# Two halves of a token operand in one matmul, and two weight rests on GpSimd, in a two-layer decoder trunk

## The chip, the cores and the metric

The kernel runs on one core of a Trainium2 chip. Its engines work in parallel, each through its own queue in order: TensorE (PE; its weight loads are listed as PEld), VectorE (DVE), ScalarE (ACT), GpSimd (POOL) and the DMA queues, which are fed from SyncE (SP), ScalarE and GpSimd. The metric is the device time of one execution in microseconds (us), taken as the median over runs.

## The reference

A residual stream of 512 tokens by 1024 channels goes through two layers. The first has a gated short convolution, the second sliding-window attention with sinks over a shared K/V; each is followed by a SwiGLU block with 2816 hidden columns. All is float32.

```python
def swiglu(h, w_gate_up, w_down):
    g, u = jnp.split(h @ w_gate_up, 2, axis=-1)
    return (jax.nn.silu(g) * u) @ w_down

for l in range(DEPTH):                     # DEPTH = 2
    if l < N_A:
        mix = short_conv_mixer(rmsnorm(h, a_pre_norm[l]), a_w_in[l], a_conv_w[l], a_w_out[l])
        h = h + rmsnorm(mix, a_post_norm[l])
    else:
        ...                                # K/V, queries, attention with sinks, b_w_o
        h = h + rmsnorm(attn, b_post_norm[j])
    ff = swiglu(rmsnorm(h, ffn_pre_norm[l]), ffn_w_gate_up[l], ffn_w_down[l])
    h = h + rmsnorm(ff, ffn_post_norm[l])
```

The change lies in the first line of `swiglu`, the product with `w_gate_up`, in both layers.

## The kernel before

**Two parts for each float.** TensorE multiplies in the rounded type fp32r. To keep float32 accuracy, each operand is split into a rounded part, made by a ScalarE copy into fp32r (`whi`, `xhi`), and the rest, made by subtracting that part from the original (`wlo`, `xlo`). `mm3` (lines 190 to 193) makes a product from three matmuls into the same PSUM bank: rounded weight by token rest (L191), rounded weight by rounded token (L192), and weight rest by rounded token (L193). Rest by rest is left out.

**Gate pairs.** The first two of the 22 tiles of hidden columns are multiplied plainly (`pgu`). The other twenty go in ten pairs per layer, twenty pairs in all. A pair is a 2 x 2 block product: the rows of blocks are gate and up, the inner index is split into two halves of 512 channels, and the tokens into two halves of 256. It is done with seven block products instead of eight, in the order 1, 2, 6, 5, 7, 3, 4 (`gate_jobs`, line 973). Each of the seven uses one 128 x 1024 weight tile (a block, or a sum of blocks) and one factor of 512 channels by 256 tokens (a half, or a sum of halves), for the two tiles e = 0, 1 of the pair and four steps k over channels: 8 calls of `mm3`, 24 matmuls of 256 columns.

Products 1, 6, 7 and 4 add up in the chain X (two PSUM banks `gx`, one for each e, 256 of 512 columns used), 5 and 3 in the chain Z (`gz`), 2 in Y (`gy`); Y and Z had two half-used banks each too. After each product and each e, `take` (lines 995 to 1014) evicts what is due into `st` and `gr`: ScalarE copies X after 1 and 6 (L1001) and Z after 5 (L1005); VectorE adds after 2 (L1003), 7 (L1007) and 3 (L1009); after 4 VectorE multiplies the up half, negated, with the gate half in `gr` (L1012, twice for each e). Between 3 and 4, `gate` applies the SiLU on ScalarE (L1036, one instruction for each e). The next product of a chain can't start in a bank before the evictions that read it are done.

The token factors are made once for each layer in `factors` (line 364): for products 1, 2 and 3 they are parts of the split tokens themselves, for 6, 5, 7 and 4 sums of token quarters, split into a rounded half (L382) and a rest half (L383) that lie beside each other in one tile of 1024 columns (`halves`).

**The line of jobs.** A layer's seven-product jobs stand in one line (`in_line`, line 471). The pairs go 0, 1, 2, then the eleven jobs of down round 0, then 3, 4, down round 1 (seven jobs), 5, 6, down round 2, 7, 8, 9, down round 3. When job j has issued its matmuls and evictions, job j + 3 is prepared (`LINE_LEAD = 3`): ScalarE rounds its weights (L466), VectorE makes the rest (L467), and the next raw tile is fetched on SP into the oldest of seven raw buffers, once that is free. So in a pair the weights of the next pair's products 1, 2 and 6 are prepared behind its products 7, 3 and 4. Four tiles each of `whi` and `wlo` go round. Behind the preparation, `issue` puts one or more DMAs on the GpSimd queue; they sum weight blocks in DRAM (`hsum`) and are paced by the rounding just made. What is left of them goes out unpaced at the pair's end (`sum_on`). In pairs 1 to 5 and 7 of each layer two of the sums are not made in DRAM but by VectorE on raw tiles (`Job.add`, L454), for products 6 and 3.

The activations of a finished pair become operands of the down rounds: `pair_sums` returns six late parts (a rounding L577 with its rest L578, sums L581 and L582, three splits L587 and L588), and one of them is issued behind each of the next jobs that are not marked `alone`. In pairs 8 and 9 `pair_acts` splits at once, behind product 4 (L1049 on ScalarE, L1050 on VectorE). Down jobs add their products into `mix` on VectorE (L636).

Each engine executes in the order written (`manual_schedule`), so a stage that waits holds up everything behind it on its engine.

Of the kernel before, what the change touches and what calls it, by code (L numbers as in the profile page):

```python
# [10 lines left out]
F32 = mybir.dt.float32  # L11
F32R = mybir.dt.float32r
AF = mybir.ActivationFunctionType
# [5 lines left out]
S = 512  # L19
# [53 lines left out]
def yoco_kernel(  # L73
# [165 lines left out]
    class Update:  # L239
# [124 lines left out]
        def factors(self):  # L364


            x = self.x[0]
            made = {p: [] for p in range(1, 8)}
            for p, k0, c in ((1, 0, 0), (2, 4, 0), (3, 4, 256)):
                made[p] = [[a[:, c : c + 256] for a in x[k0 + k]] for k in range(4)]  # L370
            for j in range(2):
                q11, q21, q12, q22 = (self.parts[i, hf, j] for hf in range(2) for i in range(2))

                nc.vector.tensor_tensor(out=q11, in0=q11, in1=q12, op=ALU.subtract)
                nc.vector.tensor_tensor(out=q12, in0=q22, in1=q12, op=ALU.subtract)
# [12 lines left out]
    class Ahead:  # L388
# [51 lines left out]
    class Job:  # L440
# [15 lines left out]
        def prepare(self):  # L456
            if not self.raws:
                return
            n = self.raws[0].n
            raw = self.raws[0].tile[:, :n]  # L460
            if self.slots:
                self.w = split_weights(None, raw, True)
                return
            hi = wsp.tile([P, D], F32R, tag="whi", name=name("whi"))
            lo = wsp.tile([P, D], F32R, tag="wlo", name=name("wlo"))
            self.begun = nc.scalar.activation(hi[:, :n], raw, AF.Copy)  # L466
            nc.vector.tensor_tensor(out=lo[:, :n], in0=raw, in1=hi[:, :n].bitcast(F32),  # L467
                                    op=ALU.subtract)
            self.w = hi, lo

# [481 lines left out]
    def ffn(l, before, ahead, gain, gpres, following):  # L952
# [20 lines left out]
        def gate_jobs(q, factors, out, to, then):  # L973

            sums = sums_of[f"g{l}{q}"]
            a21, a22, a11, a12 = (Raw(b) for b in sums.blocks)
            s1, s3, *rest = (Raw(b) for b in sums.sums)
            raws = {1: [a11], 2: [a12], 5: [s1], 7: [s3], 4: [a22]}  # L980
            if rest:
                raws[6], raws[3] = ([r] for r in rest)
            else:
                raws[6], raws[3] = [a11, s1], [a12, a11]
            chain = {1: "X", 6: "X", 7: "X", 4: "X", 5: "Z", 3: "Z", 2: "Y"}
            pools = {"X": ps_mm, "Y": ps_pt, "Z": ps_sc}
# [8 lines left out]
            def take(p, e):  # L995
                x, y, z = (banks[c][e][:, :256] if c in banks else None for c in "XYZ")
                gr = kept[2]
                g0, g1 = (gr[:, c : c + 256] for c in (e * S, e * S + 256))
                s, u = kept[e][:, :256], kept[e][:, 256:]
                if p in (1, 6):  # L1000
                    nc.scalar.activation(s, x, AF.Copy)  # L1001
                elif p == 2:
                    nc.vector.tensor_tensor(out=g0, in0=y, in1=s, op=ALU.add)  # L1003
                elif p == 5:
                    nc.scalar.activation(u, z, AF.Copy)  # L1005
                elif p == 7:
                    nc.vector.tensor_tensor(out=u, in0=x, in1=u, op=ALU.add)  # L1007
                elif p == 3:
                    nc.vector.tensor_tensor(out=g1, in0=z, in1=s, op=ALU.add)  # L1009
                else:  # L1010
                    for g, m in ((g0, x), (g1, u)):
                        nc.vector.scalar_tensor_tensor(out=g, in0=m, scalar=-1.0, in1=g,  # L1012
                                                       op0=ALU.mult, op1=ALU.mult)

            def run(p):
                def products(job):
                    if not kept:
                        kept.extend([slot("st"), slot("st"), wide("gr")])
                    whi, wlo = split[p] if p in split else job.w
                    c = chain[p]  # L1020
                    opened = c not in banks
                    if opened:
                        banks[c] = [bank("g" + c.lower(), pools[c]) for _ in range(2)]
                    for e in range(2):
                        for k in range(4):
                            kk = slice(e * S + k * P, e * S + (k + 1) * P)
                            mm3(banks[c][e][:, :256], whi[:, kk], wlo[:, kk], *factors[p][k],
                                opened and k == 0, k == 3 and p in (2, 3, 4),
                                skip_group_check=True)
                        take(p, e)  # L1030
                return products

            def gate():
                for e in range(2):
                    both = kept[2][:, e * S : (e + 1) * S]
                    nc.scalar.activation(both, both, AF.Silu)  # L1036
# [6 lines left out]
            return [Job(raws[p], run(p), {3: gate, 4: end}.get(p), len(raws[p]) > 1)  # L1043
                    for p in (1, 2, 6, 5, 7, 3, 4)]

        def pair_acts(gr, to):
            for c in (0, S):
# [543 lines left out]
```

## Time and profile before

| | |
|---|---|
| median of 3 runs | 1027.31 us (1027.06 to 1027.46) |
| the profiled execution | 1027.09 us, its span 1025.3 us |
| TensorE busy | 1016.4 us (99%), 6648 matmuls |
| VectorE busy | 823.7 us (80%), 1400 instructions |
| ScalarE busy | 577.4 us (56%), 1035 instructions |
| GpSimd busy | 195.8 us (19%), 259 instructions |
| granted TensorE clock | 0.998 of full speed |

The span runs from the first to the last instruction that the profile shows; the device time is some 2 us longer. A row of the timeline gives the start in us from the span's beginning, the duration in us, engine, line, operation, output and inputs by the program's names, shape, and how many instructions the row stands for; in brackets the idle time before it and what ended it. A row of a group gives the form, the count, the busy time in us, the mean duration in ns, and the idle time of the engine just before with what ended it. A row of a wait gives who waited, for whom, us in total, times, and the longest. A row of a window gives the stretch, its length, and for PE, PEld, DVE, ACT and POOL in turn the busy time in us and the instruction count, then the granted clock, the DMA share and GB/s. Ends of matmuls are modelled and overlap the next start, so the spacing of starts tells their cost.

### The profile page before, as it was taken

The page shows a single profiled execution, that of the slowest core. Times are in us where ns is not written, and L with a number is a line of the kernel's source. Part 1 is how long each engine was busy: PE and PEld are TensorE (multiplying, and loading weights), DVE is VectorE, ACT ScalarE, POOL GpSimd, SP SyncE. Part 2 cuts the span into 40 slices and gives each one's busy share as a digit, 9 for nine tenths or more (in the row PEclk, how much of TensorE's full clock was granted, in tenths as well). Part 3 has the DMA queues.
Part 4 walks back from the last instruction along what each step waited for, and adds up shares of the span by engine and source line. Part 5 has one row for each costly group of instructions (what it writes and reads, how often), then busy time and mean ns, then how long its engine had stood idle before and what let it go on. Part 6 is the DMA issues. An engine that isn't in the chain of part 4 may idle for free.

```text
span 1025.3 us, 17466 instructions
## 1 busy us (share of the span) xinstructions
PE 1016.4 (99%) x6648; PEld 925.8 (90%) x6648; DVE 823.7 (80%) x1400; ACT 577.4 (56%) x1035; POOL 195.8 (19%) x259
## 2 busy tenths in 40 slices
PE   9999999999999999999999999999999999999997
PEld 8888888999899898998897888889998999989986
DVE  5766767888688879878869998778886788887786
ACT  7323445865655454566476776677665554645642
POOL 0433033111111111000123653231111010110001
PEclk9999999999999999999999999999999999999999
DMA  9897699459978699779404789976889576988732
GB/s 353 293 268 224 181 255 350 135 169 291 338 246 291 200 313 319 254 220 307 164 9 156 186 246 268 233 280 153 275 282 326 167 263 208 311 286 259 243 135 83
DMA packets 66580, 244.59 MB, mean 239 GB/s; under 512 B 7872, under 2 KB 8384, under 8 KB 54720
## 3 DMA queue, kind: packets, MB, share of 16 engines
q1 hardware_dynamic: 51328, 145.98, 39.0%
q0 software_dynamic: 14592, 96.48, 36.7%
q8 instruction: 52, 0.85, 0.3%
q10 hardware_dynamic: 576, 1.02, 0.3%
q14 instruction: 32, 0.26, 0.1%
HBM read 237.15 MB, written 102.76 MB: 332 GB/s over the span
## 4 chain that ended last, share of the span: by engine, by line
PE 94%; DVE 4%; ACT 1%; DMA 1%; issue 0%; DVEq 0%; SPq 0%
PE gx L193 7%; PE gx L192 7%; PE gx L191 7%; PE gz L192 4%; PE gz L193 4%; PE gz L191 4%; PE pcub L191 4%; PE pcub L193 4%; PE pcub L192 4%; PE px L191 4%; PE px L192 4%; PE px L193 4%; PE pmix L193 3%; PE pmix L191 3%; PE pmix L192 3%; PE gy L191 2%
## 5 line engine op out<-in xcount | busy, mean ns | idle before, releaser
L467 DVE TENSOR_TENSOR wlo<-raw,whi 128x1024 fp32r<-128x1024 f32 x225 | 275.3, 1227 | 93.3 <-ACT whi L466 93.1
L466 ACT ACTIVATE whi<-raw 128x1024 fp32r<-128x1024 f32 x225 | 234.2, 1049 | 118.2 <-DVE raw L454 20.4
L192 PE MATMUL gx<-xt,whi 128*128 128x256 f32 x480 | 135.9, 283 | 0.0
L193 PE MATMUL gx<-xt,wlo 128*128 128x256 f32 x480 | 135.9, 283 | 0.0
L191 PE MATMUL gx<-xt,whi 128*128 128x256 f32 x480 | 135.9, 283 | 0.0
L192 PEld LDWEIGHTS gx<-xt,whi 128*128 128x128 f32 x480 | 92.2, 192 | 0.0
L193 PEld LDWEIGHTS gx<-xt,wlo 128*128 128x128 f32 x480 | 92.2, 192 | 0.0
L191 PEld LDWEIGHTS gx<-xt,whi 128*128 128x128 f32 x480 | 92.2, 192 | 0.0
L535 POOL DMA_DIRECT2D hsum<-in_w_gb_dram x96 | 63.5, 741 | 142.0 <-ACT whi L466 82.3
L1001 ACT ACTIVATE st<-gx 128x256 f32<-128x256 f32 x80 | 30.3, 383 | 82.6 <-PE gx L193 82.6
L535 POOL DMA_DIRECT2D hsum<-hsum x32 | 25.2, 789 | 264.3 <-ACT whi L466 209.1
L192 PE MATMUL pcub<-xhi,whi 128*128 128x512 f32 x168 | 65.4, 389 | 0.0
L191 PE MATMUL pcub<-xlo,whi 128*128 128x512 f32 x168 | 65.4, 389 | 0.0
L193 PE MATMUL pcub<-xhi,wlo 128*128 128x512 f32 x168 | 65.4, 389 | 0.0
L191 PE MATMUL px<-wlo,ahi 128*128 128x512 f32 x120 | 46.7, 390 | 0.0
L192 PE MATMUL px<-whi,ahi 128*128 128x512 f32 x120 | 46.7, 389 | 0.0
L193 PE MATMUL px<-whi,alo 128*128 128x512 f32 x120 | 46.7, 389 | 0.0
L192 PE MATMUL gz<-xt,whi 128*128 128x256 f32 x160 | 45.3, 283 | 0.0
L192 PE MATMUL gx<-xhi,whi 128*128 128x256 f32 x160 | 45.3, 283 | 0.0
L191 PE MATMUL gy<-xlo,whi 128*128 128x256 f32 x160 | 45.3, 283 | 0.0
L192 PE MATMUL gy<-xhi,whi 128*128 128x256 f32 x160 | 45.3, 283 | 0.0
L193 PE MATMUL gz<-xt,wlo 128*128 128x256 f32 x160 | 45.3, 283 | 0.0
(268 smaller groups left out, 3119.7 us busy)
## 6 DMA issues: line engine op xcount, KB each, us to landing
hsum<-in_w_gb_dram POOLq DMA_DIRECT2D x96, 512.0 KB, 8.0
raw<-hsum SPq DMA_DIRECT2D x88, 512.0 KB, 7.9
raw<-in_w_gb_dram SPq DMA_DIRECT2D x60, 512.0 KB, 7.5
hsum<-in_w_dn_dram POOLq DMA_DIRECT2D x36, 512.0 KB, 8.7
raw<-in_w_dn_dram SPq DMA_DIRECT2D x32, 512.0 KB, 6.7
hsum<-hsum POOLq DMA_DIRECT2D x28, 512.0 KB, 5.4
raw<-in_w_in_dram SPq DMA_DIRECT2D x21, 512.0 KB, 8.1
hsum<-in_w_dn_dram POOLq DMA_DIRECT2D x12, 768.0 KB, 12.7
```

The source lines that it names most:

```text
L191: nc.tensor.matmul(out, whi, xlo, start=start, stop=False, **kw)
L192: nc.tensor.matmul(out, whi, xhi, start=False, stop=False, **kw)
L193: nc.tensor.matmul(out, wlo, xhi, start=False, stop=stop, **kw)
L466: self.begun = nc.scalar.activation(hi[:, :n], raw, AF.Copy)
L467: nc.vector.tensor_tensor(out=lo[:, :n], in0=raw, in1=hi[:, :n].bitcast(F32), op=ALU.subtract)
L535: nc.gpsimd.dma_start(dst, src, max_dma_last_dim=4 * 4 * S, **kw))
L1001: nc.scalar.activation(s, x, AF.Copy)
```

## The change

In products 6, 7 and 4 the rounded token half and the rest half of a factor, which lie in one tile, are given to TensorE as one moving operand of two runs of 256 columns: one matmul with the rounded weights writes 512 columns of an X bank, the product with the rounded tokens into the first half and the product with the token rests into the second. A matmul of 256 columns with the weight rest follows. Product 1 still fills the first half only. The two halves are added when they are evicted: after 1 and 6 ScalarE copies the first half, and after 6 VectorE adds the second; after 7 VectorE adds both halves to `u` (four adds in place of two); after 4 ScalarE copies the first half, VectorE adds the second, and the multiplications follow. Chains Y and Z use one bank each for both e, their evictions are one instruction of 512 columns instead of two of 256, and so are the multiplications; the SiLU is one instruction of 1024. Evictions come once for each product, behind both e. In each pair the weight rests of the second and third job (products 2 and 6) are made by GpSimd instead of VectorE.

```diff
@@ Update.factors
                 for p, q in ((6, q22), (5, q11), (7, q12), (4, q21)):
-                    hi, lo = halves("xt", F32R)
+                    two = wide("xt", F32R)
+                    hi, lo = two[:, :S], two[:, S:]
+                    two = two.rearrange("p (i c) -> p i c", i=2)
                     nc.scalar.activation(hi, q, AF.Copy)
...
-                    made[p] += [[a[:, c : c + 256] for a in (hi, lo)] for c in (0, 256)]
+                    made[p] += [[hi[:, c : c + 256], lo[:, c : c + 256], two[:, :, c : c + 256]]
+                                for c in (0, 256)]
@@ Job
+        rest = nc.vector
...
-            nc.vector.tensor_tensor(out=lo[:, :n], in0=raw, in1=hi[:, :n].bitcast(F32),
+            self.rest.tensor_tensor(out=lo[:, :n], in0=raw, in1=hi[:, :n].bitcast(F32),
                                     op=ALU.subtract)
@@ gate_jobs
+            def take(p):
+                x, y, z = (banks.get(c) for c in "XYZ")
+                st, u, gr = kept
...
+                if p == 2:
+                    add(g0, tiles(y), tiles(st))
+                elif p == 5:
+                    nc.scalar.activation(u, z, AF.Copy)
+                elif p == 3:
+                    add(g1, tiles(z), tiles(st))
+                else:
+                    for e in range(2):
+                        a, b = x[e][:, :256], x[e][:, 256:]
+                        ste, ue = (v[:, e * 256 : (e + 1) * 256] for v in (st, u))
+                        if p == 7:
+                            add(ue, a, ue)
+                            add(ue, b, ue)
+                            continue
+                        nc.scalar.activation(ste, a, AF.Copy)
+                        if p != 1:
+                            add(ste, b, ste)
+                if p == 4:
+                    for g, m in ((g0, st), (g1, u)):
+                        nc.vector.scalar_tensor_tensor(out=g, in0=tiles(m), scalar=-1.0, in1=g,
                                                        op0=ALU.mult, op1=ALU.mult)
...
+                            if c == "X" and xboth:
+                                nc.tensor.matmul(banks[c][e], whi[:, kk], xboth[0], start=False,
+                                                 stop=False, **kw)
+                                nc.tensor.matmul(banks[c][e][:, :256], wlo[:, kk], xhi,
+                                                 start=False, stop=k == 3 and p == 4, **kw)
+                                continue
...
+                    take(p)
...
             def gate():
-                for e in range(2):
-                    both = kept[2][:, e * S : (e + 1) * S]
-                    nc.scalar.activation(both, both, AF.Silu)
+                nc.scalar.activation(kept[2], kept[2], AF.Silu)
...
+            for job in jobs[1:3]:
+                job.rest = nc.gpsimd
+            return jobs
```

More of the change, by code (lines that the diff above doesn't have):

```diff
@@ L993, in gate_jobs, with tiles, add @@
             banks, kept = {}, []
[L995 to L1003, printed above, removed]
+            def tiles(a):
+                return a.rearrange("p (e c) -> p e c", e=2)
+            def take(p):
+                x, y, z = (banks.get(c) for c in "XYZ")
+                st, u, gr = kept
+                g0, g1 = (gr.rearrange("p (e h c) -> p e h c", e=2, h=2)[:, :, h]
+                          for h in range(2))
+                def add(out, a, b):
+                    nc.vector.tensor_tensor(out=out, in0=a, in1=b, op=ALU.add)
+                if p == 2:
+                    add(g0, tiles(y), tiles(st))
                 elif p == 5:
                     nc.scalar.activation(u, z, AF.Copy)
-                elif p == 7:
-                    nc.vector.tensor_tensor(out=u, in0=x, in1=u, op=ALU.add)
                 elif p == 3:
-                    nc.vector.tensor_tensor(out=g1, in0=z, in1=s, op=ALU.add)
+                    add(g1, tiles(z), tiles(st))
                 else:
-                    for g, m in ((g0, x), (g1, u)):
-                        nc.vector.scalar_tensor_tensor(out=g, in0=m, scalar=-1.0, in1=g,
+                    for e in range(2):
[11 more added lines that the diff above has]
+                        nc.vector.scalar_tensor_tensor(out=g, in0=tiles(m), scalar=-1.0, in1=g,
                                                        op0=ALU.mult, op1=ALU.mult)
@@ L1022, in products @@
                     if opened:
-                        banks[c] = [bank("g" + c.lower(), pools[c]) for _ in range(2)]
+                        banks[c] = ([bank("gx", pools[c]) for _ in range(2)] if c == "X"
+                                    else bank("g" + c.lower(), pools[c]))
                     for e in range(2):
@@ L1026, in products @@
                             kk = slice(e * S + k * P, e * S + (k + 1) * P)
[L1027 to L1030, printed above, removed]
+                            xhi, xlo, *xboth = factors[p][k]
+                            kw = {"skip_group_check": True}
+                            if c == "X" and xboth:
[4 more added lines that the diff above has]
+                                continue
+                            out = (banks[c][e][:, :256] if c == "X"
+                                   else banks[c][:, e * 256 : (e + 1) * 256])
+                            mm3(out, whi[:, kk], wlo[:, kk], xhi, xlo,
+                                opened and k == 0 and (c == "X" or e == 0),
+                                e == 1 and k == 3 and p in (2, 3), **kw)
+                    take(p)
                 return products
             def gate():
-                for e in range(2):
-                    both = kept[2][:, e * S : (e + 1) * S]
-                    nc.scalar.activation(both, both, AF.Silu)
+                nc.scalar.activation(kept[2], kept[2], AF.Silu)
             def end():
@@ L1041, in end @@
                 return late
-            return [Job(raws[p], run(p), {3: gate, 4: end}.get(p), len(raws[p]) > 1)
+            jobs = [Job(raws[p], run(p), {3: gate, 4: end}.get(p), len(raws[p]) > 1)
                     for p in (1, 2, 6, 5, 7, 3, 4)]
+            for job in jobs[1:3]:
+                job.rest = nc.gpsimd
+            return jobs
         def pair_acts(gr, to):
```

## The prediction

> **What bounds the kernel now.** I read the page's busy times and chain first, then who waited for whom, then the start times of single instructions.
>
> ```profile
> span 1025.3 us, 17466 instructions
> ...
> PE 1016.4 (99%) x6648; PEld 925.8 (90%) x6648; DVE 823.7 (80%) x1400; ACT 577.4 (56%) x1035; POOL 195.8 (19%) x259
> ...
> PE 94%; DVE 4%; ACT 1%; DMA 1%; issue 0%; DVEq 0%; SPq 0%
> ```
>
> TensorE is busy for 99% and makes 94% of the chain. The waits of its weight loads say how little it stands still; the longest entry, and the only one on a weight rest:
>
> ```profile
> PEld psc L1273 <- issue: 4.7, 15, 0.7
> ...
> PEld px L191 <- DVE wlo L467: 0.3, 2, 0.2
> ```
>
> So a matmul taken away counts in full as long as nothing else becomes late. Busy times of matmuls overlap, so their price is read from starts (column 1):
>
> ```profile
> 408.89 0.39 PE L191 MATMUL px<-wlo,ahi 128*128 128x512 f32 x1
> ...
> 411.61 0.28 PE L191 MATMUL gx<-xlo,whi 128*128 128x256 f32 x1
> ...
> 417.36 0.28 PE L191 MATMUL gx<-xt,whi 128*128 128x256 f32 x1
> ...
> 420.24 0.28 PE L191 MATMUL gz<-xt,whi 128*128 128x256 f32 x1
> ```
>
> From 408.89 to 411.61 lie 12 products of 512 columns: 0.2267 us each. From 417.36 to 420.24 lie 24 of 256: 0.120. Two of 256 cost 0.240, 0.0133 more than one of 512.
>
> VectorE is next. In windows on gate pair 7 of layer 0 (its seven products) and on a down round:
>
> ```profile
> 411.60:431.76 20.16, 20.16 (x169) 20.14 (x168) 17.67 (x27) 12.91 (x20) 1.56 (x2) 1.00 0.81 258
> 333.16:352.23 19.07, 19.07 (x86) 15.78 (x85) 17.83 (x23) 6.37 (x6) 1.58 (x2) 1.00 0.83 262
> ```
>
> The fifth number is VectorE's busy time: 17.67 of 20.16 us. It has 2.5 us to spare in such a pair, 1.2 in a round.
>
> **The change, part by part.**
>
> ```profile
> L467 DVE TENSOR_TENSOR wlo<-raw,whi 128x1024 fp32r<-128x1024 f32 x223 | 273.9, 1232 | 93.3 <-ACT whi L466 93.1
> ...
> L192 PE MATMUL gx<-xt,whi 128*128 128x256 f32 x480 | 135.9, 283 | 0.0
> ...
> L636 DVE TENSOR_TENSOR mix<-mix,px 128x512 f32<-128x512 f32 x54 | 36.0, 685 | 5.6 <-PE px L193 5.2
> ...
> L1001 ACT ACTIVATE st<-gx 128x256 f32<-128x256 f32 x80 | 30.3, 383 | 82.6 <-PE gx L193 82.6
> ...
> L1036 ACT ACTIVATE gr<-gr 128x512 f32<-128x512 f32 x40 | 23.3, 625 | 25.7 <-DVE gr L1009 25.7
> ...
> L1003 DVE TENSOR_TENSOR gr<-gy,st 128x256 f32<-128x256 f32 x40 | 15.2, 417 | 0.0
> L582 DVE SCALAR_TENSOR_TENSOR s<-s,gr 128x256 f32<-128x256 f32 x36 | 15.2, 422 | 0.6
> ```
>
> *Products.* Products 6, 7 and 4 have 480 mm3 calls in 20 pairs (the row x480). Each loses one of its three matmuls, and 0.36 us becomes 0.2267 + 0.120: 480 x 0.0133 = **-6.4 us**. A 512-column product whose tokens come as two runs isn't in the trace; between 0.2267 (one run) and 0.240 (as two products) I take 0.2267, since it still is one instruction.
>
> *Evictions on VectorE.* Before, a pair has ten of 256 columns, two each in products 2, 7 and 3 and four in 4, at about 0.417: 4.2 us. After: 2 of 512 (0.685, L636's size), 8 adds of 256 (0.417) and 2 multiplies of 512 (0.7, some above L636) make 6.1. Against +1.9 stand two weight rests that leave, 2 x 1.23: about -0.5 us a pair, counted as nothing: it falls into the idle time above.
>
> *ScalarE.* Two more copies (2 x 0.383), one gate in place of two and one wide copy in place of two: some +0.4 us a pair beside 7 us idle. But the copies of product 4 are new ahead of the next weight rounding, which counts below.
>
> *The rests on GpSimd.* 38 of them (pair 0 has none for product 2). The page has no 128x1024 subtraction there; the same form with 512 columns, and what happens beside VectorE:
>
> ```profile
> 552.03 0.67 DVE L1213 TENSOR_TENSOR ra<-pq,ctab 128x512 f32<-128x512 f32 x1
> 552.22 1.29 POOL L1214 TENSOR_TENSOR sh<-sh,stab 128x512 f32<-128x512 f32 x1 [25.61 <-DVE sh L1211]
> ...
> 575.27 1.21 DVE L187 TENSOR_TENSOR wlo<-raw,whi 128x1024 fp32r<-128x1024 f32 x1
> ...
> 577.12 1.30 POOL L1221 TENSOR_TENSOR rlo<-ra,rhi 128x512 fp32r<-128x512 f32 x1 [2.01 <-ACT rhi L1220]
> ...
> 597.22 1.27 POOL L1214 TENSOR_TENSOR sh<-sh,stab 128x512 f32<-128x512 f32 x1 [3.93 <-DVE sh L1211]
> 597.62 1.95 DVE L187 TENSOR_TENSOR wlo<-raw,whi 128x1024 fp32r<-128x1024 f32 x1
> 598.57 2.16 POOL L1215 TENSOR_TENSOR ra<-ra,sh 128x512 f32<-128x512 f32 x1
> ```
>
> Bounds for one rest: 1.3 us and 2 x 1.30 = 2.6. I take 2.45, near the upper, for only a fixed start doesn't double. The last three rows matter most. VectorE's rest begins at 597.62 during a GpSimd product and takes 1.95 instead of 1.21: it ends 1.08 after GpSimd's end (598.49). GpSimd's next takes 2.16 instead of 1.30, for it stood behind that rest. The two exclude each other when both VectorE inputs lie in SBUF; with one in PSUM (552.03) VectorE runs at full speed.
> The Trainium skill, page "SBUF — State Buffer", section "SBUF: two separate sides", calls this port pair an exclusive lock held for a whole instruction, against VectorE operations with two SBUF inputs; these rows agree (1.95 against 1.21). By that rule the sum stays as below; without it, it would be 1027.1 - 6.4 = 1020.7.
> For the length, the Trainium skill, page "GPSIMD Engine Reference", section "Elementwise — side-by-side cycle accounting", gives 4497 ns for 2048 float32; half, 2.25, is an estimate by which the sum would be near 1027. No run here shows the size.
>
> *Where it hits.* In a pair the rests of the next pair's products 2 and 6 follow its products 3 and 4. Pair 7 to pair 8 before:
>
> ```profile
> 426.43 0.75 DVE L1007 TENSOR_TENSOR st<-gx,st 128x256 f32<-128x256 f32 x2
> 426.54 1.05 ACT L466 ACTIVATE whi<-raw 128x1024 fp32r<-128x1024 f32 x1
> 427.10 1.21 DVE L467 TENSOR_TENSOR wlo<-raw,whi 128x1024 fp32r<-128x1024 f32 x1
> ...
> 428.23 0.68 DVE L588 TENSOR_TENSOR alo<-s,ahi 128x512 fp32r<-128x512 f32 x1
> 428.83 0.75 DVE L1009 TENSOR_TENSOR gr<-gz,st 128x256 f32<-128x256 f32 x2
> 429.28 1.16 ACT L1036 ACTIVATE gr<-gr 128x512 f32<-128x512 f32 x2 [1.17 <-DVE gr L1009]
> ...
> 430.34 1.04 ACT L466 ACTIVATE whi<-raw 128x1024 fp32r<-128x1024 f32 x1
> ...
> 437.52 0.28 PE L191 MATMUL gx<-xt,whi 128*128 128x256 f32 x1
> ```
>
> After, by the same clock: the rounding of 426.54 ends at 427.7 (the wide copy ahead of it costs 0.1). GpSimd takes the port from 427.8 to 430.25, while VectorE finishes product 7's four adds (PSUM). Behind these stand product 1's rest, a split and product 3's add: the rest issues the next at 431.25, the add ends at 432.55, not 429.58. Then in line: gate to 433.6, product 4's copies to 434.2, the rounding for product 6 to 435.15, GpSimd's rest 435.25 to 437.7. Product 6 starts at 437.20 (437.52 less three savings of 0.107) and wants the rest at 437.43: **0.3 us lost**; 0.95 if the second multiply of product 4 gets the port first.
> Where the next pair also adds raw weights (1.22; pairs 1, 2, 4), VectorE goes on at 437.7: multiply 0.65, rest 1.14, split 0.35, add 0.6, rest 1.14, raw add 1.14, sums 0.85, and product 6's first add at 444.0; product 7 wants the bank at 443.15: **0.85 more**.
> From pair 8 to 9 the activations are split at once:
>
> ```profile
> 452.23 0.63 ACT L1049 ACTIVATE ahi<-gr 128x512 fp32r<-128x512 f32 x1 [0.69 <-DVE gr L1012]
> ...
> 453.58 0.36 ACT L1001 ACTIVATE st<-gx 128x256 f32<-128x256 f32 x1
> ```
>
> These two roundings wait for the blocked multiply (438.35 on that clock) and stand ahead of product 1's copies, which end 1.45 later, at 439.8; product 6 wants that bank at 437.2: **2.6 lost**.
> Per layer: 0 to 1, 1.15; 1 to 2, 0.85 (already late by then); 3 to 4, 0.6 (no split work behind pair 3); 5 to 6 and 7 to 8, 0.3 each; 8 to 9, 2.6: 5.8, and 11.6 for both.
>
> Where a down round precedes (3, 5, 7) I charge nothing:
>
> ```profile
> 352.59 1.28 DVE L636 TENSOR_TENSOR mix<-mix,px 128x512 f32<-128x512 f32 x2
> ...
> 356.67 1.23 DVE L467 TENSOR_TENSOR wlo<-raw,whi 128x1024 fp32r<-128x1024 f32 x1 [1.56 <-ACT whi L466]
> ```
>
> VectorE there works on PSUM and then idles 1.56 us for ScalarE; without this cover it would cost some 1 us each. Later raw fetches on SP (their buffers come free up to 4 us later) and the sums' issues on POOL (up to 2.5 us behind a rest) I cost at nothing: raws are fetched seven jobs ahead, some 20 us against 8 to land.
>
> **Sum.** The profiled execution took 1027.09 (span 1025.3 and 1.8 around it), 0.2 under the median. 1027.1 - 6.4 + 11.6 = **1032.3**.
>
> **Rivals.**
> *The waits stay in the slack* (faster). One quantity decides: the length of a GpSimd rest. Both rests lie on the path, so 0.1 us moves each boundary by up to 0.2. At 2.1 the waits come to some 4.4 and the gain leads by 2; at 1.3 hardly anything waits: 1021. For it: TensorE waited 0.3 in all for rests. Against: 1.30 at half the size. 1020.7 to 1025: 0.20.
> *Gain and waits cancel*, lengths of 2.1 to 2.3: 1025 to 1029: 0.15.
> *VectorE becomes the bound*: the port race goes against GpSimd at the ten boundaries with split work (+0.65 each), and the down rounds, with 1.2 us of slack, pay 1 each: 1027.1 - 6.4 + 11.6 + 6.5 + 6 = 1045. Against: 356.67's idle time. 0.09.
> *The wide product isn't cheaper* (0.240): the gain is gone, 1038.7. For it only that this operand shape isn't in the trace. 0.06.
>
> **Numbers.** My own case, 1029 to 1041, has 0.50. No change is what lies within 0.2% (2 us), about what a measurement of this kernel tells apart. Slower 0.50 + 0.09 + 0.06 = 0.65, same 0.15, faster 0.20. The range 1022 to 1046 leaves out the end of the first rival and a few cases above the third.
>
> **What the new profile would show.** Right: 480 fewer matmuls; starts 0.227 and 0.120 apart in turn; rests on POOL of some 2.45 us; VectorE rests stretched beyond 2 us beside them; weight loads or matmuls of gx waiting for POOL's rest, a VectorE add or a ScalarE copy, 10 us in all, the longest two at the last pair of each layer. Wrong: POOL rests near 2 us or less, VectorE's rests all at 1.23 us, no new TensorE wait, or weight waits on DMA.

## The result, and the profile after

| | before | after |
|---|---|---|
| median | 1027.25 us (1027.06 to 1027.46, 4 runs) | 1043.46 us (1040.87 to 1046.29, 4 runs) |
| the profiled execution, its span | 1027.09, 1025.3 us | 1042.82, 1041.0 us |
| ratio | 1 | 1.0157, interval 1.0144 to 1.0170 |
| granted clock over the span | 0.998 | 0.996 |

The changed kernel is 1.6% slower, 16.2 us by the medians, where 5 us had been forecast. Its runs also spread over 5.4 us, where those of the kernel before spread over 0.4.

The page of the kernel after: span, busy times, the chain by engine, and four groups.

```profile
span 1041.0 us, 16607 instructions
...
PE 1021.1 (98%) x6168; PEld 903.3 (87%) x6168; DVE 876.2 (84%) x1402; ACT 580.2 (56%) x1035; POOL 291.4 (28%) x297
...
PE 72%; DVE 16%; issue 4%; DMA 4%; ACT 3%; POOL 1%; DVEq 0%; ACTq 0%; POOLq 0%
...
L471 DVE TENSOR_TENSOR wlo<-raw,whi 128x1024 fp32r<-128x1024 f32 x187 | 253.3, 1360 | 51.6 <-ACT whi L470 51.5
L1049 PE MATMUL gx<-xt,whi 128*128 128x512 f32 x480 | 174.0, 401 | 5.7 <-ACT st L1025 4.5
L471 POOL TENSOR_TENSOR wlo<-raw,whi 128x1024 fp32r<-128x1024 f32 x38 | 95.8, 2522 | 226.1 <-ACT whi L470 170.0
...
L1030 DVE SCALAR_TENSOR_TENSOR gr<-st,gr 128x512 f32<-128x512 f32 x40 | 52.4, 1352 | 0.7
```

480 matmuls are gone, 6648 to 6168, and yet the span grew; TensorE's part of the chain fell from 94% to 72%, and VectorE's rose from 4% to 16%. VectorE lost 38 rests and is nevertheless busy for 876.2 us instead of 823.7: those that it kept take 1360 ns each instead of 1232.

TensorE's waits in the kernel after, where the kernel before had none on a gate product in this view (who waits, for whom, us in all, times, longest):

```profile
PE gx L1049 <- ACT st L1025: 4.5, 2, 2.3
PE gy L193 <- POOL wlo L471: 2.4, 2, 2.0
PE gx L1051 <- POOL wlo L471: 2.3, 3, 1.6
PE gx L1049 <- DVE st L1009: 1.2, 4, 0.3
```

These come to 10.4 us. The first row is the boundary from pair 8 to 9, once for each layer; the second and the 1.6 of the third are pair 7; what is left lies at the boundaries 0 to 1 and 1 to 2.

The timeline of the kernel after at the boundary 8 to 9 of layer 0:

```profile
457.02 1.06 ACT L1063 ACTIVATE gr<-gr 128x1024 f32<-128x1024 f32 x1 [4.28 <-DVE gr L1009]
...
457.99 0.64 ACT L1025 ACTIVATE st<-gx 128x256 f32<-128x256 f32 x2
...
458.51 1.06 ACT L470 ACTIVATE whi<-raw 128x1024 fp32r<-128x1024 f32 x1
...
459.65 2.48 POOL L471 TENSOR_TENSOR wlo<-raw,whi 128x1024 fp32r<-128x1024 f32 x1 [4.95 <-ACT whi L470]
...
459.78 2.89 DVE L1030 SCALAR_TENSOR_TENSOR gr<-st,gr 128x512 f32<-128x512 f32 x1
...
462.76 1.15 ACT L1079 ACTIVATE ahi<-gr 128x512 fp32r<-128x512 f32 x2 [3.19 <-DVE gr L1030]
...
463.82 0.64 ACT L1025 ACTIVATE st<-gx 128x256 f32<-128x256 f32 x2
...
464.24 0.50 PE L1049 MATMUL gx<-xt,whi 128*128 128x512 f32 x1 [2.25 <-ACT st L1025]
```

It is the chain of the prediction. GpSimd's rest starts 0.13 us ahead of the second multiply of product 4; that multiply takes 2.89 and ends 0.5 behind the rest; the two roundings of the activations, which need it, idle for 3.19; product 1's copies stand behind them, and TensorE stands still for 2.25 us for the bank.

The same kernel at pair 7 of layer 0, which the prediction charged with nothing:

```profile
412.83 1.06 ACT L470 ACTIVATE whi<-raw 128x1024 fp32r<-128x1024 f32 x1 [3.43 <-DMA raw<-in_w_gb_dram]
...
413.93 1.23 DVE L458 TENSOR_TENSOR raw<-raw,raw 128x1024 f32<-128x1024 f32 x1 [2.08 <-DMA raw<-hsum]
414.02 5.69 POOL L471 TENSOR_TENSOR wlo<-raw,whi 128x1024 fp32r<-128x1024 f32 x2 [10.44 <-ACT whi L470]
...
417.43 0.39 PE L193 MATMUL gy<-xhi,wlo 128*128 128x256 f32 x1 [2.02 <-POOL wlo L471]
...
417.85 2.94 DVE L471 TENSOR_TENSOR wlo<-raw,whi 128x1024 fp32r<-128x1024 f32 x1 [1.50 <-ACT whi L470]
```

The pair's first matmul starts at 412.13. The weights of its product 2 are rounded from 412.83 on, since their raw tile landed only then. VectorE's sum of raw tiles holds the port from 413.93, so GpSimd's rest, issued at 414.02, is finished at 417.4, and product 2, which wants it at 415.24, waits.

Windows of the kernel after (stretch, its length, busy time and count of PE, PEld, DVE, ACT and POOL, granted clock, DMA share, GB/s): the whole of pair 7 of layer 0 and the down round that answers to the one shown of before, and then three times two stretches of 3.41 us.

```profile
412.13:435.83 23.70, 21.68 (x145) 20.39 (x144) 18.57 (x23) 11.58 (x17) 9.60 (x5) 0.93 0.75 243
333.80:352.85 19.05, 19.05 (x86) 15.78 (x85) 18.80 (x26) 7.85 (x10) 4.48 (x3) 1.00 0.88 282
...
414.78:418.19 3.41, 1.39 (x12) 1.18 (x11) 1.91 (x4) 2.92 (x6) 3.41 (x2) 1.00 0.62 255
418.19:421.60 3.41, 3.41 (x18) 3.41 (x18) 2.94 (x2) 0.88 (x1) 3.04 (x3) 0.50 0.19 22
...
462.56:465.97 3.41, 1.73 (x9) 1.52 (x10) 1.93 (x4) 3.21 (x6) 0.00 (x0) 1.00 0.50 167
465.97:469.38 3.41, 3.41 (x27) 3.25 (x26) 3.41 (x6) 2.08 (x5) 0.00 (x0) 1.00 0.80 255
974.56:977.97 3.41, 1.50 (x9) 1.33 (x10) 1.93 (x4) 2.98 (x6) 0.00 (x0) 1.00 0.43 155
977.97:981.38 3.41, 3.41 (x15) 3.02 (x14) 3.16 (x5) 1.58 (x4) 0.00 (x0) 0.50 0.75 259
```

Pair 7 takes 23.70 us instead of 20.16; the down round takes as long as before (19.05, 19.07). Behind the wait of pair 7 the granted clock is 0.50 for 3.41 us: TensorE is busy all through, and its matmuls of 256 columns start 0.213 us apart instead of 0.120. The same happens behind the wait of pair 9 in layer 1 (977.97), and not behind that of layer 0 (465.97: clock 1.00), though that wait is no shorter.

The windows show what differs. In all profiles of this case the clock changes only at whole multiples of 3.413 us from its first change (the two drops here lie 559.78 us apart, 164 times as much). Of the wait in pair 7 2.02 us fall into one such stretch (3.41 less 1.39 busy), of that in pair 9 of layer 1 1.91, but of that in layer 0 only 1.68, for it lies across two stretches. In the profiles of the two kernels and of the experiments below there are ten such drops, and one at the end of each; every one follows a stretch with 1.82 us or more of idle TensorE, and no stretch with 1.78 or less is followed by one.

**Where the 15.7 us of span come from**, by the starts of the stages in the two profiles, layer 0 and layer 1 together:

| | us |
|---|---|
| 20 pairs, 20.00 us instead of 20.16 where nothing waits (2.9 of it in products 6, 7 and 4: 60 x 0.048) | -3.2 |
| boundaries 0 to 1 (0.99, 1.30) and 1 to 2 (0.53, 0.50) | +3.3 |
| boundary 3 to 4 | 0 |
| boundaries 5 to 6 and 7 to 8, 0.23 each | +0.9 |
| boundary 8 to 9 (2.5 each, 2.41 of it ahead of product 6) | +5.0 |
| pair 7 behind the down round (3.71, 2.44), 1.6 of it the low clock in layer 0 | +6.15 |
| low clock behind 8 to 9 of layer 1 | +1.5 |
| the two layer ends | +2.1 |
| start of the first pair, and the down rounds between | -0.2 |
| sum | 15.6 |

### The profile page after: what moved, and what is told of

It is laid out like the page before. It is cut to its first block, busy times and chain, and to the rows that moved or that the text cites. A ratio compares the mean times of both kernels' runs of the same rounds, so it can differ in the third digit from the quotient of the medians.

```text
span 1041.0 us, 16607 instructions
## 1 busy us (share of the span) xinstructions
PE 1021.1 (98%) x6168; PEld 903.3 (87%) x6168; DVE 876.2 (84%) x1402; ACT 580.2 (56%) x1035; POOL 291.4 (28%) x297
## 4 chain that ended last, share of the span: by engine, by line
PE 72%; DVE 16%; issue 4%; DMA 4%; ACT 3%; POOL 1%; DVEq 0%; ACTq 0%; POOLq 0%
PE gx L1049 7%; DVE wlo L471 4%; PE gx L1051 4%; DMA raw<-in_w_gb_dram 4%; PE pcub L191 4%; PE pcub L193 4%; PE pcub L192 4%; PE px L191 3%; PE px L193 3%; PE px L192 3%; PE gz L193 3%; PE gz L192 2%; PE gz L191 2%; PE pmix L191 2%; PE pmix L192 2%
## 5 line engine op out<-in xcount | busy, mean ns | idle before, releaser
L471 DVE TENSOR_TENSOR wlo<-raw,whi 128x1024 fp32r<-128x1024 f32 x187 | 253.3, 1360 | 51.6 <-ACT whi L470 51.5
L1049 PE MATMUL gx<-xt,whi 128*128 128x512 f32 x480 | 174.0, 401 | 5.7 <-ACT st L1025 4.5
L471 POOL TENSOR_TENSOR wlo<-raw,whi 128x1024 fp32r<-128x1024 f32 x38 | 95.8, 2522 | 226.1 <-ACT whi L470 170.0
L1049 PEld LDWEIGHTS gx<-xt,whi 128*128 128x128 f32 x480 | 90.9, 189 | 26.0 <-ACT st L1025 4.9
L1009 DVE TENSOR_TENSOR st<-gx,st 128x256 f32<-128x256 f32 x160 | 62.1, 419 | 7.5 <-ACT st L1025 6.1
L1063 ACT ACTIVATE gr<-gr 128x1024 f32<-128x1024 f32 x20 | 21.3, 1063 | 72.9 <-DVE gr L1009 72.9
L1025 ACT ACTIVATE st<-gx 128x256 f32<-128x256 f32 x120 | 40.8, 379 | 37.7 <-PE gx L1051 17.4
L1030 DVE SCALAR_TENSOR_TENSOR gr<-st,gr 128x512 f32<-128x512 f32 x40 | 52.4, 1352 | 0.7
L297 POOL TENSOR_TENSOR ur<-uv,mhalf 128x1 f32<-128x1 f32 x15 | 14.0, 930 | 128.3 <-DVE uv L293 128.1
L193 PE MATMUL gy<-xhi,wlo 128*128 128x256 f32 x160 | 46.2, 289 | 2.4 <-POOL wlo L471 2.4
```

The lines of the kernel that those rows point to most:

```text
L193: nc.tensor.matmul(out, wlo, xhi, start=False, stop=stop, **kw)
L471: self.rest.tensor_tensor(out=lo[:, :n], in0=raw, in1=hi[:, :n].bitcast(F32), op=ALU.subtract)
L1009: nc.vector.tensor_tensor(out=out, in0=a, in1=b, op=ALU.add)
L1025: nc.scalar.activation(ste, a, AF.Copy)
L1030: nc.vector.scalar_tensor_tensor(out=g, in0=tiles(m), scalar=-1.0, in1=g, op0=ALU.mult, op1=ALU.mult)
L1049: nc.tensor.matmul(banks[c][e], whi[:, kk], xboth[0], start=False, stop=False, **kw)
```

## The experiments

The theory was the prediction's own: the loss is time that product matmuls wait, because GpSimd's rests are long and shut VectorE out. Its rivals: that the wide product itself costs more than thought, by its two runs or by what stands ahead of it; that late raw tiles and not the rests make pair 7; that the evictions, which are longer now, do it. Each experiment starts from the kernel after unless it says otherwise. The medians of the kernel before beside them were 1027.44 to 1027.54 us.

**The products alone.** All rests go back to VectorE.

```diff
-            for job in jobs[1:3]:
-                job.rest = nc.gpsimd
```

> The changed kernel with all weight rests back on VectorE; everything else as changed. Theory A (the GpSimd rests make all the new waits): 480 products save 0.36 - 0.354 us each as the changed trace spaces them, about -2.8 us, and the evictions cost nothing: 1024.4. Theory B (the evictions grouped behind both e, and the copies of product 4 ahead of the next rounding, already make TensorE wait): 1030 or more, with waits of gx on a ScalarE copy or a VectorE add.

Measured: 1026.4 us (1025.73 to 1026.56, 10 runs), ratio 0.9988 (0.9978 to 0.9997). In its waits no gate product is left. Its groups, and the starts of product 6 in pair 0 (from the first of it to the first of product 5, which follows):

```profile
L471 DVE TENSOR_TENSOR wlo<-raw,whi 128x1024 fp32r<-128x1024 f32 x225 | 274.5, 1226 | 64.2 <-ACT whi L470 64.1
L1030 DVE SCALAR_TENSOR_TENSOR gr<-st,gr 128x512 f32<-128x512 f32 x40 | 25.9, 688 | 0.7
```
```profile
209.67 0.40 PE L1049 MATMUL gx<-xt,whi 128*128 128x512 f32 x1
209.90 0.28 PE L1051 MATMUL gx<-xt,wlo 128*128 128x256 f32 x1
...
212.50 0.28 PE L191 MATMUL gz<-xt,whi 128*128 128x256 f32 x1
```

Eight steps take 2.83 us, 0.354 each, and not the 0.347 of the prediction (0.2267 and 0.120). A step is a wide matmul of 0.237 and one of 256 of 0.118. The gain of the products is 1.1 us in this kernel, and the change of place of 38 rests costs 17. The gain is less than the 2.8 expected because the layer ends lose 2.0 us here too. The multiply of product 4 takes 688 ns here and 1352 in the kernel after, where it waits for the port.

**The rests alone.** The kernel before, with GpSimd making the same rests.

```diff
...
+            for job in jobs[1:3]:
+                job.rest = nc.gpsimd
...
```

> The kernel before with only one edit: the weight rests of products 2 and 6 of each pair on GpSimd. Theory A: the same waits at pair 7 and at pairs 8 to 9 as in the changed kernel, though the path over product 4 is shorter: 1032 to 1040. Theory B: 1027, within 0.2% of before, since the rests then stay in the slack.

Measured: 1029.93 us (1028.56 to 1032.0, 10 runs), ratio 1.0026 (1.0016 to 1.0035): +2.4 us. The products alone give -1.1, the rests alone +2.4, both +16.2. The parts don't add up. The rests are as long here:

```profile
L468 POOL TENSOR_TENSOR wlo<-raw,whi 128x1024 fp32r<-128x1024 f32 x38 | 99.0, 2606 | 201.0 <-ACT whi L467 140.3
```

and in the profiled execution, the fastest of the ten (1028.56), TensorE waited for one of them once, 0.3 us. The median lies between the two times expected. The old order has 34.9 us less work on VectorE (823.7 against 858.6 in the kernel with the products alone), and no ScalarE copy between product 4 and the next rounding. So the length of GpSimd's rest by itself is not what costs; it costs where the products' part of the change has already taken the slack. Which of the two differences takes it isn't separated here.

**One run of 512 columns.** The products alone, with the rounded and rest columns of a step side by side, so that the wide product's tokens are one run.

```diff
-                    hi, lo = two[:, :S], two[:, S:]
+                    halves_of = two.rearrange("p (k i c) -> p i k c", k=2, i=2)
+                    hi, lo = halves_of[:, 0], halves_of[:, 1]
...
```

> As e1_products_only, but a factor's rounded and rest columns for one step lie side by side, so that the 512-column operand is one run. If two runs make the product dearer (0.2345 against 0.2267 us in the traces), starts come 0.2267 apart and the time is 3.5 us below e1, near 1021. If the dearer product comes from following a 256-column one, the spacing stays at 0.234 and the time is that of e1.

Measured: 1026.3 us (1025.76 to 1026.93, 10 runs), ratio 0.9989 (0.9980 to 0.9998). Product 6 of pair 0 in its timeline, from its first matmul to the first of product 5:

```profile
210.41 0.40 PE L1050 MATMUL gx<-xt,whi 128*128 128x512 f32 x1
...
213.25 0.28 PE L191 MATMUL gz<-xt,whi 128*128 128x256 f32 x1
```

Eight steps take 2.84 us. The price is the same, so the two runs aren't its cause. A product of 512 takes 0.2267 behind another of 512, as in the down rounds, and 0.237 in turn with one of 256 (mean of the starts of all 480; the expectation had read 0.2345). Single changes between the two sizes don't show this: before, where a down round follows product 4, a 512 behind a 256 took 0.233, and where a pair follows, a 256 behind a 512 took 0.113, together no more than the prediction's 0.2267 + 0.120. Why taking turns costs 0.008 more for each step stays open.

**No rests on GpSimd for pairs 7 and 9.**

```diff
             for job in jobs[1:3]:
-                job.rest = nc.gpsimd
+                if q not in (7, 9):
+                    job.rest = nc.gpsimd
```

> The changed kernel with the rests of pairs 7 and 9 of each layer back on VectorE (8 of 38 rests). If those rests themselves cost the large waits (product 2 and 6 of pair 7, product 6 of pair 9, and the low clock after them), some 11 to 12 us go: about 1031. If pair 7 waits because raw weights land late, whoever makes the rests, only pair 9's part goes (2.4 us in each layer and 1.5 of low clock): about 1037.

Measured: 1032.48 us (1031.78 to 1033.01), ratio 1.0048 (1.0032 to 1.0065). Eight of 38 rests moved back take 11.0 us of the 16.2 away, and the spread falls to 1.2 us. The two places hold two thirds of the loss; the boundaries 0 to 1 and 1 to 2 stay in its waits with 2.0 us.

**No rests on GpSimd for pair 7.**

```diff
-                job.rest = nc.gpsimd
+                if q != 7:
+                    job.rest = nc.gpsimd
```

> The changed kernel with pair 7's two rests in each layer on VectorE, all others on GpSimd. If the waits at pair 7 (2.2 us, and 0.4 with 1.6, and 1.5 of low clock) come from its own GpSimd rests, about 6 us go: 1037. If they come from raw weights that land late because earlier rests held the raw buffers, the waits stay: 1042.

Measured: 1039.04 us (1037.09 to 1039.99), ratio 1.0111 (1.0096 to 1.0126): 4.4 us less than after. Its waits, and the window with the wait of pair 9 in layer 0 and the one behind it:

```profile
PE gx L1049 <- ACT st L1025: 4.5, 2, 2.2
...
PE gx L1051 <- DVE wlo L471: 0.7, 2, 0.4
```
```profile
457.93:461.34 3.41, 1.16 (x11) 0.96 (x9) 2.65 (x3) 1.51 (x4) 1.26 (x1) 1.00 0.23 76
461.34:464.75 3.41, 3.41 (x11) 2.93 (x12) 2.70 (x4) 2.38 (x4) 0.00 (x0) 0.50 0.61 232
```

The wait of `gy` on GpSimd is gone. But the raw tile still comes late here: product 2's weights are rounded 0.43 us behind the pair's first matmul (412.38), released by the transfer, as the timeline has it:

```profile
412.81 1.06 ACT L470 ACTIVATE whi<-raw 128x1024 fp32r<-128x1024 f32 x1 [2.60 <-DMA raw<-in_w_gb_dram]
```

What is left of pair 7's waits is 0.7 us in both layers together, for VectorE's rest; by the starts the pair loses 0.8 and 1.1 us. So a late tile with VectorE's rests behind it costs 1.9 us; with GpSimd's rests in their place it is 6.15, the low clock with it. The wait of 2.2 us at pair 9 of layer 0, after which the kernel after had clock 1.00, lies here in one stretch (2.25 us idle) and is followed by 0.50.

**No rests on GpSimd for pair 6.** The rests of pair 6 are made ahead of down round 2. If they hold up the fetches, then pair 7's tiles come earlier without them.

```diff
-                job.rest = nc.gpsimd
+                if q != 6:
+                    job.rest = nc.gpsimd
```

> The changed kernel with pair 6's two rests in each layer on VectorE. If rests made one pair earlier hold raw buffers, so that pair 7's raw weights are fetched late, the waits at pair 7 go: about 1037. If they come from pair 7's own rests, only the small waits from pair 5 to 6 go (0.25 us each): 1043.

Measured: 1041.32 us (1039.4 to 1045.2), ratio 1.0140 (1.0118 to 1.0162). Pair 7's loss falls only in part, to 2.05 and 1.46 in the two layers, and the whole by 2.1 us, within the spread of both. How much pair 6's rests add to the lateness isn't settled.

**The activations of pair 8 later.** Their splits are issued behind product 2 of pair 9 instead of behind product 4, so that product 1's copies don't queue behind them.

```diff
-            for c in (0, S):
+            def part(c):
...
+            return [lambda: None, lambda: (part(0), part(S))]
```

> The changed kernel, but the two activation splits behind pair 8 are issued behind product 2 of pair 9 instead of at once. If ScalarE, held by those splits, makes product 6 of pair 9 wait for product 1's copies (2.4 us in each layer, and a lower clock after it in one), 5 to 6 us go: about 1037.5. If the GpSimd rest of product 6 would come as late anyway, another wait takes the place: 1041 or more.

Measured: 1035.58 us (1034.88 to 1038.81), ratio 1.0086 (1.0069 to 1.0102). The wait of `gx` on ScalarE is gone from the waits, and 7.9 us with it; 4.8 of them are the boundary itself in the table, and the low clock behind it goes with it (1.5). In this kernel pair 9's rests are still on GpSimd: the queue of ScalarE carried the loss, as the prediction had it. The wait that stays is pair 7's:

```profile
PE gy L193 <- POOL wlo L471: 4.5, 2, 2.7
```

**Product 4's evictions behind the rounding.** They are issued at the pair's end, so that the next rounding doesn't wait for the two new copies.

```diff
-                    take(p)
+                    if p != 4:
+                        take(p)
...
             def end():
+                take(4)
```

> The changed kernel, but product 4's evictions are issued behind the preparation of the job three ahead, so that ScalarE rounds product 6's weights before it copies product 4's halves. If the rest of product 6 is late because that rounding stands behind the copies (1.5 us), the waits of product 6 from 0 to 1 and 8 to 9 shrink: 1033 to 1038. If the port and the rests' length set the time, it stays within 2 us of the changed kernel.

Measured: 1043.81 us (1042.48 to 1045.89), ratio 1.0166 (1.0149 to 1.0183): no better. It starts GpSimd's rest earlier and the multiplies later, so a multiply waits for the port all the same (1.93 us at pair 9 of layer 0); in its profile the waits on ScalarE at pair 9 are 4.4 us, and 1.8 us on a down round's weight rest are new.

**One of the two rests.** Only product 2's, and only product 6's.

```diff
-            for job in jobs[1:3]:
+            for job in jobs[1:2]:
```

> The changed kernel with only the rest of product 2 of each pair on GpSimd (18 rests), product 6's back on VectorE. If the wait from pair 8 to 9 comes from product 6's rest holding the port against product 4's multiplications, it goes (2 x 2.4 us and the low clock), and half of the waits at pair 7: about 1031. If the two rests only add up, half of the 17 us against e1 stays: 1035.

```diff
-            for job in jobs[1:3]:
+            for job in jobs[2:3]:
```

> The changed kernel with only the rest of product 6 on GpSimd (20 rests). If that rest, last on the path over product 4, makes the wait from pair 8 to 9 alone, these 2.4 us in each layer stay and the waits of 0 to 1, 1 to 2 and of product 2 in pair 7 go: about 1033. If the wait needs both rests, it shrinks: 1029 or less.

Measured: 1031.72 us (1031.14 to 1032.04), ratio 1.0042 (1.0025 to 1.0059) for product 2's; 1029.53 us (1028.58 to 1031.84), ratio 1.0021 (1.0011 to 1.0032) for product 6's. Against the products alone these are +5.3 and +3.1, and both together +17.1: 8.6 us belong to neither by itself. At the boundary 8 to 9 the rest of product 6 alone costs 0.73 for each layer, where both cost 2.4. Product 2's rest alone leaves a wait of 1.9 us for GpSimd at pair 7 of layer 1; by the starts pair 7 loses 1.2 and 3.6 us with it, the second with a low clock behind the wait. With product 6's alone pair 7 loses nothing, but there product 2's raw tile also came early, 1.5 us ahead of the pair.

**A spare GpSimd instruction.** The products alone, all rests on VectorE, and at the places of the two rests a GpSimd subtraction of 960 columns on a tile that nothing reads, released by the same rounding.

```diff
-                job.rest = nc.gpsimd
+                job.idle = True
...
+            if self.idle:
+                made = nc.gpsimd.tensor_tensor(out=spare, in0=spare, in1=spare, op=ALU.subtract)
```

> As e1_products_only (all weight rests on VectorE), but GpSimd makes, at the places of the two rests, a subtraction of 960 columns in SBUF on a tile of its own that nobody reads (some 2.4 us, released by the same rounding); one slot buffer fewer, for room. If the port lock against VectorE is a cost of its own, VectorE's rests and multiplications beside it stretch past 2 us and TensorE waits from pair 8 to 9: 1031 to 1035. If only the lateness of the rests costs, the time is that of e1, 1026.4.

Measured: 1046.83 us (1045.11 to 1047.35), ratio 1.0187 (1.0172 to 1.0202). The groups and the waits of this kernel:

```profile
L474 DVE TENSOR_TENSOR wlo<-raw,whi 128x1024 fp32r<-128x1024 f32 x225 | 292.4, 1307 | 48.0 <-ACT whi L473 47.8
...
L477 POOL TENSOR_TENSOR spare<-spare 128x960 f32<-128x960 f32 x38 | 83.5, 2196 | 236.3 <-ACT whi L473 236.3
```
```profile
PE gx L1060 <- DVE wlo L474: 10.3, 8, 1.9
PE gx L1058 <- ACT st L1034: 2.7, 2, 1.3
```

Nothing reads what the spare instruction makes, and still the kernel is 20.4 us slower than the products alone, more than the 5 to 9 us expected. TensorE now waits for VectorE's rests, 10.3 us, and at pair 9 for ScalarE, 2.7 us. So the exclusion costs without any rest being made late by GpSimd itself. The amount is not its alone: this kernel also has one slot buffer fewer (42 instead of 43), it fills the spare tile once on VectorE, and sums that GpSimd issues stand behind the spare instruction. 1.3 us are lost ahead of the first pair, before a spare instruction runs; the rest wasn't separated. In the kernel after, VectorE has 38 rests fewer, so the two amounts don't compare.

**The products alone, with both late edits** (the activations of pair 8 and product 4's evictions).

> A try for the best: the wide products with all rests on VectorE, product 4's evictions behind the preparation of the job three ahead, and pair 8's activation splits behind product 2 of pair 9. If e1's rest of the loss is in the last pair's evictions, 1025 to 1026; if those were hidden, e1's 1026.4.

Measured: 1028.85 us (1028.55 to 1030.53, 10 runs), ratio 1.0015 (1.0005 to 1.0024): 2.4 us slower than the products alone, with 1.8 us of waits for a down round's weight rest, as in the kernel that moved product 4's evictions. That misses both expectations. The best kernels are the products alone, with two runs or with one (1026.4 and 1026.3), some 0.12% under the kernel before, which is within what the prediction counts as no change.

## Why the prediction was right and wrong

The direction was right, and so was the mechanism at the boundaries between pairs. The size was not: +5.0 us forecast, +16.2 measured, above the 1029 to 1041 of its own case though inside the wide range.

- *The matmuls that go, and the waits.* 480 went. "10 us in all" was the sum of waits that the profile would show, and they are 10.4. That the sums agree is luck: 4.0 of the 10.4 lie at pair 7, where none was charged, and the other boundaries wait less than forecast.
- *"Products", -6.4 us: mis-sized.* The working took the lower of its two bounds, 0.2267, since a product of 512 "still is one instruction". Measured in turn with a product of 256 it is 0.237, close to the upper bound of 0.240, and 0.118 for the one that follows. A product of eight steps takes 2.832 us instead of 24 x 0.120 = 2.88, 0.048 less and not 0.107: 60 x 0.048 = 2.9 us. Both prices had been read in rows of equal products. This is 3.5 us of the 11.2 that were missed.
- *"Where a down round precedes (3, 5, 7) I charge nothing": false for pair 7*, 6.15 us, the largest miss. The view of VectorE's idle time at pair 5 was taken for all three. Pair 7 differs in its transfers: before the change already the rounding of product 1's weights idled 4.05 us for a raw tile:

```profile
406.04 1.06 ACT L466 ACTIVATE whi<-raw 128x1024 fp32r<-128x1024 f32 x1 [4.05 <-DMA raw<-in_w_gb_dram]
```

  (timeline of the kernel before; the pair starts at 411.61). The step that failed is "raw fetches I cost at nothing: raws are fetched seven jobs ahead, some 20 us against 8 to land". The fetch of product 2's tile was issued 20.1 us ahead of pair 7, as said, but here it took 17.5 us to land before the change, 18.6 with the products alone and 19.5 after; and with the wide products it is issued 18.9 us ahead. The time from issue to landing of this one transfer, before and after:

```profile
DMA to landing us min/median/max: 17.5/17.5/17.5
...
DMA to landing us min/median/max: 19.5/19.5/19.5
```

  So in layer 0 product 2's weights were rounded 2.44 us ahead of the pair's first matmul before, 0.26 ahead with the products alone, and 0.70 behind it after. Without rests on GpSimd for this pair the tile is as late and the pair loses 1.9 us in both layers, so most of the 6.15 is the long rest behind the late tile. Why the tiles land later, and differently from run to run, stays open; putting pair 6's rests back on VectorE helped too little to name them.
- *8 to 9, 2.6 for each layer: right*, 2.41 ahead of product 6 and 2.5 in all. Two experiments on this place agree: taking pair 9's rests off GpSimd beside pair 7's (1039.04 to 1032.48), and moving the activations out of ScalarE's queue.
- *The other boundaries: right in kind, some too high.* 0 to 1 was 1.15 and measured 0.99 and 1.30; 1 to 2 0.85, measured 0.5; 3 to 4 0.6, measured 0; 5 to 6 and 7 to 8 0.3, measured 0.23. With 8 to 9 they make 9.3 of the 11.6.
- *The length of GpSimd's rest, 2.45: right.* Where it needn't wait it takes 2.40 (the row below, layer 1), on average 2.52 with its own waits for the port.

```profile
926.81 2.40 POOL L471 TENSOR_TENSOR wlo<-raw,whi 128x1024 fp32r<-128x1024 f32 x1 [10.28 <-ACT whi L470]
```

  The Trainium skill, page "GPSIMD Engine Reference", section "Elementwise — side-by-side cycle accounting", gives 4497 ns for 2048 float32. Half of that was the estimate 2.25; the trace has 2.40, and the measurement decides.
- *VectorE, "about -0.5 us a pair, counted as nothing": the instructions were right, the busy time not.* The evictions and factors added 34.9 us to VectorE in 20 pairs (products alone against before), 1.75 a pair where 1.9 had been worked out. But with 38 rests of 1.226 gone from 858.6, VectorE should be busy for 812.0 and is busy for 876.2: 64 us, 1.7 for each GpSimd rest, in which its instructions were waiting for the port. The exclusion that the prediction used at three places shows at 33 of the 38 rests, where a VectorE instruction with two SBUF inputs is stretched beside GpSimd's; the spare instruction shows the same where nothing depends on GpSimd. The Trainium skill, page "SBUF — State Buffer", section "SBUF: two separate sides", calls the shared port an exclusive lock for a whole instruction. The runs agree, also for the multiply (688 to 1352 ns).
- *Not in the prediction at all:* the low clock behind two waits, some 3 us together, and the layer ends, 2.1 us, nearly all of which the products alone have too (1.2 and 0.7: waits for the normed tokens and for down round 3's weights, and 0.26 in the last two products of pair 9).
- *The rivals.* "VectorE becomes the bound" came nearest in time (1045), but by the wrong place: the down rounds, which it charged with 1 us each, take 19.05 us, no longer than before. "The wide product isn't cheaper" (1038.7) was right to 0.003 us for each wide product, with a chance of 0.06. "The waits stay in the slack" and "cancel" are excluded by the 10.4 us.
- That the runs spread over 5.4 us instead of 0.4 fits waits on transfers and on the granted clock; without pairs 7 and 9 the spread is 1.2. The trigger of the spread was not isolated.

## What to carry to other kernels

Before work is moved from VectorE to GpSimd, count what VectorE does with two SBUF inputs just behind the place: an instruction there waits for GpSimd's whole instruction, and whoever queues behind it on a third engine pays, so a loaded VectorE can become busier by losing work. Read the price of a matmul from a row of the order in which it will stand, not from a run of equal ones. And a place is safe because its own rows show slack: look at each boundary, at the transfers ahead of it too, before one of them is taken for the others.

## What the runs showed of the hardware

- A 512-column fp32r matmul starts 0.2267 us after another of 512, and takes 0.237 in turn with matmuls of 256 that take 0.118. One run of columns or two makes no difference (2.84 and 2.83 us for eight steps).
- A GpSimd subtraction of 128 x 1024 float32 takes 2.40 us where it needn't wait; one of 960 columns of a tile from itself 2.196 on average. A VectorE instruction with two SBUF inputs that falls into it ends behind it: 2.94 us for a rest of 1.23, 2.89 for a multiply of 0.69.
- The granted clock fell to 0.50 for 3.41 us behind some waits of TensorE of about 2 us (418.19, 977.97), and not behind another of 2.25 (464.24). What tells them apart in these profiles is how much of the wait lies in one of the fixed stretches of 3.41 us: 1.82 us or more were followed by the low clock, 1.78 or less were not. One such stretch cost 1.5 to 1.6 us.
